# Row groups of the matmul array in a decoder trunk's mixer: neighbouring small matmuls put on different row groups and different banks

## The chip, the cores and the metric

One Trainium2 chip, one NeuronCore of it. The metric is device time in microseconds (us), the median of several executions. Engines are named as in the profile: PE is TensorE (matmul), PEld its weight load, DVE is VectorE, ACT is ScalarE, POOL is GpSimd, SP is SyncE, which issues most DMAs.

## What is computed

Two layers, each a mixer (RWKV-7 heads beside a pooling mixer) and a PEER expert FFN, on 512 tokens of width 1024. Only the mixer's recurrence matters here. Cut down, for each of 8 heads of size 64:

```python
def rwkv7_step(state, inp):
    r_t, w_t, k_t, v_t, kk_t, a_t = inp
    sa = jnp.einsum('bhvk,bhk->bhv', state, -kk_t)
    state = (state * w_t[:, :, None, :]
             + sa[..., None] * (kk_t * a_t)[:, :, None, :]
             + v_t[..., None] * k_t[:, :, None, :])
    y = jnp.einsum('bhvk,bhk->bhv', state, r_t)
    return state, y
_, ys = lax.scan(rwkv7_step, s0, (rh, wh, kh, vh, kk, ah))
```

## The kernel before

The kernel does not step through 512 tokens. It cuts them into 16 chunks of 32 (CH) and treats each chunk in closed form. Two heads of 64 rows share a tile of 128 partitions; such a pair is handled by `pair(p)`, p = 0 to 3. Four groups of 128 tokens (t = 0 to 3, NT = 4) each hold four chunks (cc = 0 to 3), one to each 32 partitions.

All matmuls named here have float32 operands; the profile shows two records of MATMUL for each. A matmul whose operands lie on 64 or 32 of the 128 partitions uses only those rows of the array (its row group); one whose output has 64 partitions uses only those columns. The steps that the change touches:

- **Triangular inputs** (L446 to L465). For each pair p and head h four matmuls of 64 rows (L454) fill one bank of PSUM; ACT (h = 0) and DVE (h = 1) copy its diagonal blocks out, and a DMA takes them to the forward substitution on DVE (L474 to L494).
- **Gram products** (`gram`, L618). Called for "ak", "rb" and "rkm", once for each head: four matmuls of 64 rows into one bank, then one masked DVE multiply (L625). Head 0 lies on rows 0 to 63, head 1 on rows 64 to 127.
- **Transitions** (`gmat(cc)`, L654). Once for each cc: four matmuls of 32 rows (row group cc) into one bank, then one DVE multiply (L661).
- **Chunk inputs** (`hmat(cc)`, L664). Once for each cc: eight matmuls of 64 rows and 64 columns into one bank, the two heads on different columns, then one ACT copy (L674). Rows 0 to 63 serve cc 0 and 1, rows 64 to 127 cc 2 and 3.
- Around them stand matmuls on all 128 rows: `transposed` (L601), `xm` (L632), `wu` (L641), `ypart` (L683, L684), and the recurrence over chunks, `chain(c)` (L694): one matmul (L703) and two DVE instructions (L704, L705) per step, 15 steps one after the other for each pair (14 with a matmul). `yout` (L708) has small 64x64 matmuls of its own.

Banks come from a pool of five ("ps"), a pool of two ("pss", every fourth request of `bank2`), and one for the chain ("psc").

The order of the work is set twice. The program writes it with `zipped`, which deals several lists of blocks out in proportion: the second part of pair p's blocks beside the chain of pair p-1, the output of pair p-2, the first part of pair p+1 and steps that accumulate the adaLN modulation on DVE (L197, eight instructions for each step). PRE = 12 says how many blocks of a pair make up its first part. Then the framework's scheduler orders the instructions on each engine (`schedule_with_timeline_sim=True`). [...]

Of the kernel before, what the change touches and what calls it, by code (L numbers as in the profile page):

```python
# [9 lines left out]
F32 = mybir.dt.float32  # L10
# [4 lines left out]
AF = mybir.ActivationFunctionType  # L15
ALU = mybir.AluOpType
# [3 lines left out]
P = 128  # L20
T = 512
NT = T // P
# [3 lines left out]
CH = 32  # L26
# [19 lines left out]
GEND = 4  # L46
PO = 1
FN, FM, FS = 3, 18, 8
PRE, EARLY = 12, True
G8B = 3  # L50
EG = 6
NROW = 6
# [56 lines left out]
def body(ctx, tc, A, tap=None):  # L109
    nc = tc.nc  # L110
    V, S, G, TE = nc.vector, nc.scalar, nc.gpsimd, nc.tensor
# [17 lines left out]
    def bank(shape=(P, T)):  # L129
        return psp[0].tile(list(shape), F32, tag="ps", name=nm("ps"))  # L130
# [4 lines left out]
    def s2t(name, shape=(P, T), dt=F32):  # L135
        return s2.tile(list(shape), dt, tag="s2", name=nm(name))

    def hht(name, shape=(P, T), dt=F32R):
        return hh.tile(list(shape), dt, tag="hh", name=nm(name))
# [9 lines left out]
    def C(n):  # L149
        o, w = COFF[n]  # L150
        return const[:, o:o + w]
# [8 lines left out]
    for l in range(L):  # L160
        v = pers.tile([P, NVEC], F32, name=f"vec{l}")
# [156 lines left out]
    def mixer(l):  # L318
        with ExitStack() as mctx:
# [79 lines left out]
            for t in range(NT):  # L399
                pt = bank()  # L400
# [44 lines left out]
                V.tensor_tensor(Pi, k, Pi, op=ALU.mult)  # L445
            for p in range(4):  # L446
                a, at = bt_[p], at_[p]
                for h in range(2):
                    hr = slice(h * 64, (h + 1) * 64)
                    hd = 2 * p + h  # L450
                    pt = bank((P, NT, P))
                    for t in range(NT):
                        ts_ = slice(t * P, (t + 1) * P)
                        TE.matmul(pt[:, t], at[hr, ts_], a[hr, ts_], start=True, stop=True)  # L454
                    for cc in range(4):
                        rows = slice(cc * CH, (cc + 1) * CH)
                        if h == 0:
                            S.activation(acmp[hd // 4][rows, hd % 4], pt[rows, :, rows], AF.Copy)
                        else:
                            V.tensor_copy(acmp[hd // 4][rows, hd % 4], pt[rows, :, rows])  # L460
                if p % 2 == 1:
                    for cc in range(4):
                        rows = slice(cc * CH, (cc + 1) * CH)
                        nc.sync.dma_start(ascr[cc, (p // 2) * 16:(p // 2 + 1) * 16].rearrange("i t s -> t i s"),
                                          acmp[p // 2][rows].rearrange("t h n s -> t (h n) s"))  # L465
# [101 lines left out]
            def bank2(shape=(P, T)):  # L567
                nb[0] += 1
                return sbank(shape) if nb[0] % 4 == 0 and not apart[0] else psp[0].tile(list(shape), F32, tag="ps", name=nm("ps"))
# [4 lines left out]
            def pair(p):  # L574
# [3 lines left out]
                z = {}  # L578
# [3 lines left out]
                def scaled(n, src):  # L582
                    def f():
                        if n == 0:
                            z["bk"] = [s2t("bk") for _ in range(2)]
                        pc = PC[:, p].rearrange("p (q s) -> p q s", s=2)
                        for j in range(2):
                            V.tensor_tensor(pairs(z["bk"][j])[:, :, j ^ n], pairs(src)[:, :, j], pc[:, :, j].unsqueeze(2).to_broadcast([P, NCH // 2, CH]), op=ALU.mult)
                    return f
# [6 lines left out]
                def transposed(n, src, outs=None):  # L596
                    def f():
                        s_ = z["bk"][n[1]] if n[0] == "bk" else z["vs"] if n == "UV" else src
                        pt = bank2((P, NT, P))
                        for t in range(NT):  # L600
                            TE.transpose(pt[:, t], s_[:, t * P:(t + 1) * P], ident)  # L601
                        if n == "AX":
                            for h in range(2):
                                z["AX", h] = q3("AX")
                                S.activation(z["AX", h][:, :, hrs[1 - h]], pt[:, :, hrs[h]], AF.Copy)
                        elif n == "vT":
                            for h in range(2):
                                S.activation(vz[p % 2][:, :, P * h:P * h + 64], pt[:, :, hrs[h]], AF.Copy)
                        elif n == "UV":
                            z[n] = [q3("UV") for _ in range(2)]  # L610
                            for j in range(2):
                                S.activation(z[n][j], pt, AF.Copy)
                        else:
                            z[n] = q3(n)
                            S.activation(z[n], pt, AF.Copy)
                    return f

                def gram(n, h, lh, rh, mk):  # L618
                    def f():
                        pt = bank2((P, NT, P))  # L620
                        for t in range(NT):
                            ts_ = slice(t * P, (t + 1) * P)
                            TE.matmul(pt[:, t], lh[hrs[h], ts_], rh[hrs[h], ts_], start=True, stop=True)
                        z[n, h] = hht(n, (P, NT, P), F32)
                        V.tensor_tensor(z[n, h], pt, C(mk).unsqueeze(1).to_broadcast([P, NT, P]), op=ALU.mult)  # L625
                    return f

                def xm(h):
# [7 lines left out]
                def wu(g):  # L636
                    def f():
                        pw = bank2((P, 2, 2, P))
                        for t in range(2):
                            for h in range(2):  # L640
                                TE.matmul(pw[:, t, h], Fb[:, 2 * p + h, 2 * g + t], z["AX", h][:, 2 * g + t], start=True, stop=True)  # L641
                        z["WU", g] = w = s2t("WU", (P, 2, 2, P))
                        beat[0] = S.activation(w, pw, AF.Copy)
                        u = w.rearrange("p t h c -> p t (h c)").rearrange("p t (b c) -> p t b c", c=64)[:, :, 0:4:3]
                        for cc in range(4):
                            rows = slice(cc * CH, (cc + 1) * CH)
                            out = z["UV"][cc % 2][rows, 2 * g:2 * g + 2].rearrange("p t (h c) -> p t h c", c=64)
                            (UENG[cc])(out, u[rows])
                    return f

                def W(t):
                    return z["WU", t // 2][:, t % 2].rearrange("p h c -> p (h c)")[:, 64:192]

                def gmat(cc):  # L654
                    def f():
                        rows = slice(cc * CH, (cc + 1) * CH)
                        pg = bank2((P, NT, P))
                        for t in range(NT):
                            TE.matmul(pg[:, t], W(t)[rows], z["bk", cc % 2][rows, t], start=True, stop=True, tile_position=(cc * CH, 0))
                        z["G", cc] = q3("G")  # L660
                        V.tensor_tensor(z["G", cc], pg, C("bones").unsqueeze(1).to_broadcast([P, NT, P]), op=ALU.mult)  # L661
                    return f

                def hmat(cc):  # L664
                    def f():
                        rows = slice(cc // 2 * 64, cc // 2 * 64 + 64)
                        ph = bank2((P, NT, 64))
                        for t in range(NT):
                            for h in range(2):
                                hr = hrs[h]  # L670
                                TE.matmul(ph[hr, t], z["bk", cc % 2][rows, t, hr], z["UV"][cc % 2][rows, t, hr], start=True, stop=True, tile_position=(cc // 2 * 64, h * 64))
                        if cc % 2 == 0:
                            z["H", cc // 2] = s2t("H", (P, 2, NT, 64))
                        S.activation(z["H", cc // 2][:, cc % 2], ph, AF.Copy)  # L674
                    return f

                def ypart(h):
                    def f():
# [3 lines left out]
                        for t in range(NT):  # L682
# [3 lines left out]
                        V.tensor_tensor(n3(rt)[hrs[h]], py[hrs[1 - h]], n3(rt)[hrs[h]], op=ALU.add)  # L686
                    return f

                blocks = [scaled(0, bt), scaled(1, kt), swapped, transposed("vT", v), gram("ak", 0, kt, at, "lt"), gram("ak", 1, kt, at, "lt"),
                          transposed("AX", at), transposed("UV", None), transposed(("bk", 0), None), transposed(("bk", 1), None), xm(0), xm(1),  # L690
                          gram("rb", 0, bt, rt, "le"), gram("rb", 1, bt, rt, "le"),
                          gram("rkm", 0, kt, rt, "le"), gram("rkm", 1, kt, rt, "le"), wu(0), wu(1), gmat(0), hmat(0), gmat(1), hmat(1), gmat(2), hmat(2), gmat(3), hmat(3), ypart(0), ypart(1)]

                def chain(c):  # L694
                    def f():
# [616 lines left out]
```

## Time and profile before

| what | value |
|---|---|
| median of 3 runs | 3503.16 us (3496.99 to 3510.04) |
| the profiled execution | 3505.42 us, its span 3503.7 us |
| mean granted PE clock | 0.94 of full |
| busy in the span | PE 94%, PEld 82%, DVE 80%, ACT 40%, POOL 25% |
| mixer of layer 0, from the triangular inputs to the last chain step | 131.7 to 413.5 us |
| mixer of layer 1, the same | 1852.1 to 2135.9 us |
| steps touched (L623, L659, L671) at work | 164 to 377 us and 1908 to 2094 us |

The page is of one execution. Time between the span and the run's own time (1.7 us) lies around the program. A matmul's end is modelled, so this text goes by the starts: the time from a matmul's start to the start of the next one of its list.

### The profile page before, as it was taken

Reading aid. Unit: us, or ns where it says so; the run is one execution under the profiler, and the core shown is the slowest. Engines: PE = TensorE matmul, PEld = TensorE weight load, DVE = VectorE, ACT = ScalarE, POOL = GpSimd, SP = SyncE. Lnnn points to the kernel's source line nnn. Section 1 sums busy time; section 2 is a strip of 40 time slices with the busy share of each in tenths; the row PEclk is TensorE's granted clock in tenths of the full one; section 3 lists DMA queues with packets and bytes.
Section 4 is the critical chain, followed back from the end, with each engine's and each line's share of the span. In section 5 each row is a group of like instructions: output and inputs, shape, how many; then the busy total and the mean of one; then the engine's idle time right before and its main releaser. Section 6 shows DMA issues by size and latency. Waiting matters only on the chain. (4 is left out here: it accounts for less than half of the span.)

```text
span 3503.7 us, 51112 instructions
## 1 busy us (share of the span) xinstructions
PE 3280.4 (94%) x18154; PEld 2870.3 (82%) x18154; DVE 2814.1 (80%) x6227; ACT 1389.2 (40%) x2228; POOL 869.7 (25%) x684
## 2 busy tenths in 40 slices
PE   5899898999999999999899998999999999999997
PEld 3778677999998888888777876889999888889886
DVE  5666479998877888899939654999898688888888
ACT  4433132345573334333353422334556543333333
POOL 2000000432202222556500000023331122245554
PEclk7977799999999999999999878999999999999998
DMA  5213244567789999999922232335767999999996
GB/s 192 76 55 99 72 163 139 154 196 262 265 289 354 334 343 347 356 381 399 360 72 85 73 97 83 119 118 161 265 238 276 325 327 343 339 341 355 350 369 260
DMA packets 361377, 826.41 MB, mean 236 GB/s; under 512 B 46496, under 2 KB 189600, under 8 KB 357792
## 3 DMA queue, kind: packets, MB, share of 16 engines
q1 hardware_dynamic: 287392, 554.68, 46.9%
q0 software_dynamic: 73728, 268.47, 20.3%
q8 instruction: 142, 2.33, 0.3%
q14 instruction: 115, 0.94, 0.1%
HBM read 730.75 MB, written 92.27 MB: 235 GB/s over the span
## 5 line engine op out<-in xcount | busy, mean ns | idle before, releaser
L277 PE MATMUL pss<-hi,wsp 128*128 128x384 f32 (+1 forms) x5168 | 1075.9, 359 | 97.0 <-DVE wsp L260 34.3
L1159 PE MATMUL ps<-vv,wg 128*128 128x512 f32 x4608 | 1078.8, 393 | 21.9 <-ACT vv L1142 6.8
L277 PEld LDWEIGHTS pss<-hi,wsp 128*128 128x128 f32 x5168 | 935.7, 194 | 171.6 <-DVE wsp L260 46.8
L1159 PEld LDWEIGHTS ps<-vv,wg 128*128 128x128 f32 x4608 | 867.3, 189 | 207.3 <-ACT vv L1142 11.4
L259 ACT ACTIVATE wsp<-raw 128x1024 fp32r<-128x1024 f32 x341 | 359.8, 1057 | 519.6 <-PE pss L277 409.1
L277 PE MATMUL pss<-lo,wsp 128*128 128x384 f32 (+1 forms) x2584 | 533.5, 347 | 0.0
L852 POOL DMA_INDIRECT row<-u,ex x256 | 314.3, 1228 | 845.7 <-DVE row L858 643.3
L260 DVE TENSOR_TENSOR wsp<-raw,wsp 128x1024 fp32r<-128x1024 f32 x341 | 431.6, 1267 | 67.2 <-ACT wsp L259 66.6
L277 PEld LDWEIGHTS pss<-lo,wsp 128*128 128x128 f32 x2584 | 461.4, 188 | 22.0 <-issue 0.5
L852 POOL DMA_INDIRECT row<-v,ex x256 | 332.2, 1298 | 243.9 <-DVE ox L866 191.6
L1143 DVE TENSOR_TENSOR vv<-raw,vv 128x512 fp32r<-128x512 f32 x512 | 345.1, 691 | 46.6 <-ACT vv L1142 42.0
L1142 ACT ACTIVATE vv<-raw 128x512 fp32r<-128x512 f32 x512 | 291.4, 619 | 112.2 <-DMA raw<-v 71.2
L858 DVE SCALAR_TENSOR_TENSOR row<-row,hx 128x1024 f32<-128x1024 f32 x256 | 318.0, 1248 | 13.9 <-DMA row<-u,ex 13.8
L866 DVE SCALAR_TENSOR_TENSOR ox<-row,wx,ox 128x1024 f32<-128x1024 f32 x254 | 325.1, 1280 | 2.5
L1133 ACT ACTIVATE wg<-ge 128x384 fp32r<-128x384 f32 x256 | 132.9, 524 | 487.9 <-DVE ge L1131 202.2
L968 POOL TENSOR_TENSOR eq<-eq,cid 128x400 f32<-128x400 f32 x128 | 181.6, 1438 | 478.4 <-DVE eq L966 341.2
L934 POOL TENSOR_TENSOR hf<-hi,lo 128x128 f32<-128x128 f32 x16 | 9.8, 624 | 991.3 <-DMA ada<-ada 923.6
L1134 DVE TENSOR_TENSOR wg<-ge,wg 128x384 fp32r<-128x384 f32 x256 | 141.0, 554 | 106.7 <-ACT wg L1133 94.4
L1043 ACT ACTIVATE gb<-ps 128x512 f32<-128x512 f32 x192 | 199.3, 1162 | 0.0
L1131 DVE TENSOR_TENSOR ge<-ge,g 128x192 f32<-128x192 f32 x496 | 156.7, 352 | 40.3 <-DMA g<-gscr 29.9
L1126 ACT ACTIVATE ge<-pss 128x384 f32<-128x384 f32 x80 | 39.2, 490 | 259.3 <-PE pss L277 255.1
L1022 DVE TENSOR_TENSOR oh<-oh,selg 128x1024 f16<-128x1024 f16 x96 | 71.1, 740 | 47.5 <-PE ps L1041 47.2
(451 smaller groups left out, 3307.6 us busy)
## 6 DMA issues: line engine op xcount, KB each, us to landing
raw<-uT SPq DMA_DIRECT2D x256, 512.0 KB
raw<-v SPq DMA_DIRECT2D x256, 512.0 KB
gscr<-gb SPq DMA_DIRECT2D x24, 2048.0 KB
g<-gscr SPq DMA_DIRECT2D x124, 384.0 KB
gespill<-ge SPq DMA_DIRECT2D x176, 192.0 KB
ge<-gespill SPq DMA_DIRECT2D x176, 192.0 KB
ada<-ada SPq DMA_DIRECT2D x96, 256.0 KB
raw<-ada SPq DMA_DIRECT2D x48, 512.0 KB
```

The costliest lines, as they stand in the source:

```text
L259: S.activation(w[:, 0], raw, AF.Copy)
L260: V.tensor_tensor(w[:, 1], raw, w[:, 0].bitcast(F32), op=ALU.subtract)
L277: TE.matmul(pt, w[:, a, k * P:(k + 1) * P], hs[k][b], start=start and n == 0, stop=stop and n == len(steps) - 1)
L852: G.indirect_dma_start(out=rows[n], out_offset=None, in_=A["u" if n < P else "v"], in_offset=bass.IndirectOffsetOnAxis(ap=ex[:, n % P:n % ...
L858: V.scalar_tensor_tensor(row, row, 1.0, hx, op0=ALU.mult, op1=ALU.mult, accum_out=dots[:, e:e + 1])
L866: V.scalar_tensor_tensor(ox, row, wx[:, e:e + 1], ox, op0=ALU.mult, op1=ALU.add)
L968: pace["G"] = G.tensor_tensor(eq, eq, z["id"][:, h].unsqueeze(1).to_broadcast([P, 8, NC]), op=ALU.mult)
L1043: S.activation(gb[:, :, o:o + 4].rearrange("p i t -> p t i"), pt, AF.Copy, scale=1.0 / GSC)
L1131: V.tensor_tensor(gq, gq, g[:, :, c % IG], op=ALU.mult)
L1142: S.activation(vv[0][q], raw[:, q * T:(q + 1) * T], AF.Copy)
L1143: vlo[q] = V.tensor_tensor(vv[1][q], raw[:, q * T:(q + 1) * T], vv[0][q].bitcast(F32), op=ALU.subtract)
L1159: end[0] = TE.matmul(acc[t][d2], wg[a][:, ts_], vv[b][d2], start=(c == 0 and a == 0 and b == 0), stop=(c == NK - 1 and a == 1))
```

## The change

The three kinds of products and the triangular inputs take all their banks first and then go over t with the heads (or the chunks) innermost, so that a matmul and the next one in the program use different row groups and different banks. `gram` does both heads in one block, `gmat` all four cc in one block, `hmat(s)` the two row halves b for one s (cc = 2b + s). The list of blocks is shorter by this (20 entries, not 28), and PRE goes from 12 to 11, which cuts the list at the same place as before. The number of matmuls, copies and DVE multiplies is the same, as are their shapes.

```diff
-PRE, EARLY = 12, True
+PRE, EARLY = 11, True
...
             for p in range(4):
                 a, at = bt_[p], at_[p]
+                both = [bank((P, NT, P)) for _ in range(2)]
+                for t in range(NT):
+                    ts_ = slice(t * P, (t + 1) * P)
+                    for h in range(2):
+                        hr = slice(h * 64, (h + 1) * 64)
+                        TE.matmul(both[h][:, t], at[hr, ts_], a[hr, ts_], start=True, stop=True)
                 for h in range(2):
-                    hr = slice(h * 64, (h + 1) * 64)
                     hd = 2 * p + h
-                    pt = bank((P, NT, P))
-                    for t in range(NT):
-                        ts_ = slice(t * P, (t + 1) * P)
-                        TE.matmul(pt[:, t], at[hr, ts_], a[hr, ts_], start=True, stop=True)
...
-                def gram(n, h, lh, rh, mk):
+                def gram(n, lh, rh, mk):
                     def f():
-                        pt = bank2((P, NT, P))
+                        pts = [bank2((P, NT, P)) for _ in range(2)]
                         for t in range(NT):
                             ts_ = slice(t * P, (t + 1) * P)
-                            TE.matmul(pt[:, t], lh[hrs[h], ts_], rh[hrs[h], ts_], start=True, stop=True)
-                        z[n, h] = hht(n, (P, NT, P), F32)
-                        V.tensor_tensor(z[n, h], pt, C(mk).unsqueeze(1).to_broadcast([P, NT, P]), op=ALU.mult)
+                            for h in range(2):
+                                TE.matmul(pts[h][:, t], lh[hrs[h], ts_], rh[hrs[h], ts_], start=True, stop=True)
+                        for h in range(2):
+                            z[n, h] = hht(n, (P, NT, P), F32)
+                            V.tensor_tensor(z[n, h], pts[h], C(mk).unsqueeze(1).to_broadcast([P, NT, P]), op=ALU.mult)
                     return f
...
-                def gmat(cc):
+                def gmat():
+                    pgs = [bank2((P, NT, P)) for _ in range(4)]
+                    for t in range(NT):
+                        for cc in range(4):
+                            rows = slice(cc * CH, (cc + 1) * CH)
+                            TE.matmul(pgs[cc][:, t], W(t)[rows], z["bk", cc % 2][rows, t], start=True, stop=True, tile_position=(cc * CH, 0))
+                    for cc in range(4):
+                        z["G", cc] = q3("G")
+                        V.tensor_tensor(z["G", cc], pgs[cc], C("bones").unsqueeze(1).to_broadcast([P, NT, P]), op=ALU.mult)
+
+                def hmat(s):
                     def f():
...
+                        phs = [bank2((P, NT, 64)) for _ in range(2)]
                         for t in range(NT):
...
+                            for b in range(2):
+                                rows = hrs[b]
+                                for h in range(2):
+                                    TE.matmul(phs[b][hrs[h], t], z["bk", s][rows, t, hrs[h]], z["UV"][s][rows, t, hrs[h]], start=True, stop=True, tile_position=(b * 64, h * 64))
```

What the scheduler makes of it is seen in the order of the instructions. **PE, layer 0, the Gram products rb and rkm of pair 0**, ahead of `wu` (rt, bt, kt are the tiles of r, b and k; ps and pss are banks). Before:

```order
L632 MATMUL ps_1507<-vz_394,ak_1467 128x64 x4
L623 MATMUL ps_1513<-rt_400,bt_445 128x128 x4
L623 MATMUL pss_1520<-rt_400,bt_445 128x128 x4
L623 MATMUL ps_1527<-rt_400,kt_576 128x128 x4
L623 MATMUL ps_1534<-rt_400,kt_576 128x128 x4
L641 MATMUL ps_1541<-AX_1400,Fb 128x128
```

and after:

```order
L635 MATMUL ps_1507<-vz_394,ak_1467 128x64 x4
L625 MATMUL ps_1513<-rt_400,bt_445 128x128
L625 MATMUL pss_1514<-rt_400,bt_445 128x128
L625 MATMUL ps_1513<-rt_400,bt_445 128x128
L625 MATMUL pss_1514<-rt_400,bt_445 128x128
L625 MATMUL ps_1513<-rt_400,bt_445 128x128
L625 MATMUL pss_1514<-rt_400,bt_445 128x128
L625 MATMUL ps_1513<-rt_400,bt_445 128x128
L625 MATMUL pss_1514<-rt_400,bt_445 128x128
L625 MATMUL ps_1527<-rt_400,kt_576 128x128
L625 MATMUL ps_1528<-rt_400,kt_576 128x128
```

Four matmuls of one head, then four of the other, have become head by head. Not everywhere: rb and rkm of pair 3 and ak of pairs 0 and 1 still stand as x4 and x4 in the new order of layer 0.

**PE, layer 0, transitions and chunk inputs of pair 0**, right behind `wu` (WU is its result, bk the scaled keys, UV the chunk's values). Before:

```order
L659 MATMUL ps_1563<-('bk', 0)243_1418,WU_1546 128x128 x2
L671 MATMUL ps_1570<-UV_1409,('bk', 0)243_1418 64x64 x4
L659 MATMUL ps_1581<-('bk', 1)245_1425,WU_1546 128x128 x2
L659 MATMUL ps_1598<-('bk', 0)243_1418,WU_1546 128x128 x2
L671 MATMUL pss_1588<-UV_1410,('bk', 1)245_1425 64x64 x4
L671 MATMUL ps_1605<-UV_1409,('bk', 0)243_1418 64x64 x4
L659 MATMUL ps_1563<-('bk', 0)243_1418,WU_1557 128x128 x2
L659 MATMUL ps_1581<-('bk', 1)245_1425,WU_1557 128x128 x2
L659 MATMUL ps_1598<-('bk', 0)243_1418,WU_1557 128x128 x2
```

and after:

```order
L662 MATMUL pss_1586<-('bk', 1)245_1425,WU_1546 128x128 x2
L674 MATMUL ps_1563<-UV_1409,('bk', 0)243_1418 64x64 x4
L674 MATMUL ps_1564<-UV_1409,('bk', 0)243_1418 64x64 x4
L662 MATMUL ps_1585<-('bk', 0)243_1418,WU_1546 128x128
L662 MATMUL ps_1587<-('bk', 0)243_1418,WU_1546 128x128
L662 MATMUL ps_1588<-('bk', 1)245_1425,WU_1546 128x128
L662 MATMUL ps_1585<-('bk', 0)243_1418,WU_1546 128x128
L662 MATMUL ps_1587<-('bk', 0)243_1418,WU_1546 128x128
L662 MATMUL ps_1588<-('bk', 1)245_1425,WU_1546 128x128
```

The scheduler had already mixed the two kinds before the change; now they change places less often, and three or four row groups follow each other one matmul at a time.

**DVE, layer 0, the masked copies of pair 1's transitions** (G<-ps), beside the chain of pair 0 (M, H) and an accumulation of the modulation (acc). Before:

```order
L661 TENSOR_TENSOR G_1746<-ps_1741,const 128x512
L195 TENSOR_SCALAR acc_1781<-raw_1782,silu_c 128x512
L661 TENSOR_TENSOR G_1803<-ps_1798,const 128x512
L197 SCALAR_TENSOR_TENSOR acc_1781<-raw_1782,silu_c,acc_1781 128x512
L705 TENSOR_TENSOR M_1670<-H_1579,psc_1730 128x64
```

and after:

```order
L708 TENSOR_TENSOR M_1657<-H_1583,psc_1763 128x64
L195 TENSOR_SCALAR acc_1767<-raw_1768,silu_c 128x512
L665 TENSOR_TENSOR G_1839<-ps_1819,const 128x512
L707 SCALAR_TENSOR_TENSOR H_1581<-M_1657,PC,H_1581 128x64
L665 TENSOR_TENSOR G_1841<-pss_1820,const 128x512
L665 TENSOR_TENSOR G_1843<-ps_1821,const 128x512
L665 TENSOR_TENSOR G_1845<-ps_1822,const 128x512
L197 SCALAR_TENSOR_TENSOR acc_1767<-raw_1768,silu_c,acc_1767 128x512
L708 TENSOR_TENSOR M_1657<-H_1581,psc_1806 128x64
```

Before, two of the four copies stood here and the other two 15 rows later; now all four stand together, with a step of the chain (M) behind them. On POOL nothing moves. On SP a few weight loads move by a few places, and on DVE some rows of the layer's later stages change places; the instructions themselves are the same.

More of the change, by code (lines that the diff above doesn't have):

```diff
@@ L457, in mixer @@
                         if h == 0:
-                            S.activation(acmp[hd // 4][rows, hd % 4], pt[rows, :, rows], AF.Copy)
+                            S.activation(acmp[hd // 4][rows, hd % 4], both[h][rows, :, rows], AF.Copy)
                         else:
-                            V.tensor_copy(acmp[hd // 4][rows, hd % 4], pt[rows, :, rows])
+                            V.tensor_copy(acmp[hd // 4][rows, hd % 4], both[h][rows, :, rows])
                 if p % 2 == 1:
@@ L655, in f @@
+                def hmat(s):
                     def f():
-                        rows = slice(cc * CH, (cc + 1) * CH)
-                        pg = bank2((P, NT, P))
+                        phs = [bank2((P, NT, 64)) for _ in range(2)]
                         for t in range(NT):
-                            TE.matmul(pg[:, t], W(t)[rows], z["bk", cc % 2][rows, t], start=True, stop=True, tile_position=(cc * CH, 0))
-                        z["G", cc] = q3("G")
-                        V.tensor_tensor(z["G", cc], pg, C("bones").unsqueeze(1).to_broadcast([P, NT, P]), op=ALU.mult)
@@ L662, in gmat @@
[L662 to L674, printed above, removed]
+                            for b in range(2):
+                                rows = hrs[b]
+                                for h in range(2):
+                                    TE.matmul(phs[b][hrs[h], t], z["bk", s][rows, t, hrs[h]], z["UV"][s][rows, t, hrs[h]], start=True, stop=True, tile_position=(b * 64, h * 64))
@@ L675, in hmat @@
+                        for b in range(2):
+                            if s == 0:
+                                z["H", b] = s2t("H", (P, 2, NT, 64))
+                            S.activation(z["H", b][:, s], phs[b], AF.Copy)
                     return f
@@ L687, in ypart @@
                     return f
-                blocks = [scaled(0, bt), scaled(1, kt), swapped, transposed("vT", v), gram("ak", 0, kt, at, "lt"), gram("ak", 1, kt, at, "lt"),
+                blocks = [scaled(0, bt), scaled(1, kt), swapped, transposed("vT", v), gram("ak", kt, at, "lt"),
                           transposed("AX", at), transposed("UV", None), transposed(("bk", 0), None), transposed(("bk", 1), None), xm(0), xm(1),
-                          gram("rb", 0, bt, rt, "le"), gram("rb", 1, bt, rt, "le"),
-                          gram("rkm", 0, kt, rt, "le"), gram("rkm", 1, kt, rt, "le"), wu(0), wu(1), gmat(0), hmat(0), gmat(1), hmat(1), gmat(2), hmat(2), gmat(3), hmat(3), ypart(0), ypart(1)]
+                          gram("rb", bt, rt, "le"), gram("rkm", kt, rt, "le"), wu(0), wu(1), hmat(0), gmat, hmat(1), ypart(0), ypart(1)]
                 def chain(c):
```

## Prediction

> **What bounds the kernel now.** First the page: how busy PE is, and the slices of the span with the granted clock.
>
> ```profile
> PE 3280.4 (94%) x18154; PEld 2870.3 (82%) x18154; DVE 2814.1 (80%) x6227; ACT 1389.2 (40%) x2228; POOL 869.7 (25%) x684
> PE   5899898999999999999899998999999999999997
> PEclk7977799999999999999999878999999999999998
> ```
>
> PE is the busiest engine, and the clock is low where the mixers stand: in slices 3 to 5 of 88 us each, and in slices 23 to 25 for layer 1. Next the table by stretches, from the first `wu` to the last products of pair 3 and on to the output projection, for both layers (columns: stretch, length, PE, PEld, DVE, ACT, POOL busy, then granted clock, DMA share, GB/s), and two short stretches inside the first.
>
> ```profile
> 226.00:384.00 158.00, 154.94 (x1134) 130.83 (x1133) 90.31 (x204) 48.05 (x107) 0.00 (x0) 0.73 0.26 83
> 384.00:428.00 44.00, 36.00 (x245) 26.93 (x243) 19.84 (x51) 5.41 (x10) 0.00 (x0) 0.81 0.05 17
> 1950.00:2103.00 153.00, 150.21 (x1142) 126.65 (x1142) 89.42 (x204) 49.49 (x110) 0.00 (x0) 0.77 0.28 85
> 236.00:257.00 21.00, 20.94 (x240) 18.35 (x239) 12.08 (x27) 12.25 (x30) 0.00 (x0) 0.99 0.01 2
> 291.00:311.00 20.00, 20.00 (x98) 15.19 (x97) 9.38 (x19) 2.35 (x6) 0.00 (x0) 0.50 0.25 79
> ```
>
> In these 158 and 153 us PE is busy for 98%, DVE for 57%, ACT for 30%. The clock is not 0.73: it is 0.99 or 0.50 by turns, and a mean in between. Who waits for whom from 226 to 384 us (us in total, times, longest):
>
> ```profile
> ACT H L674 <- PE ps L671: 29.0, 11, 5.3
> DVE M L705 <- PE psc L703: 21.5, 20, 3.8
> DVE G L661 <- PE ps L659: 9.1, 3, 5.7
> PE psc L703 <- DVE M L705: 3.0, 9, 0.5
> ```
>
> DVE and ACT wait for PE; PE waits 3.0 us in all. So PE's own list sets the time of this stage, and what it is spared there comes off the end, as far as the clock holds and no new wait comes.
>
> **How PE takes small matmuls.** The timeline of PE (start, length, line, xcount of records, two for each matmul): the triangular inputs of pairs 0 and 1, of pair 2, then Gram products, `gmat` and `hmat` of pair 0 at full clock, and one `gmat` alone at half clock.
>
> ```profile
> 131.70 2.82 PE L454 MATMUL ps<-bt,at 64*128 64x128 f32 x32
> 134.60 3.94 PE L277 MATMUL pss<-hi,wsp 128*128 128x512 f32 x16
> 140.28 1.71 PE L454 MATMUL ps<-bt,at 64*128 64x128 f32 x16
> 141.92 1.42 PE L277 MATMUL pss<-hi,wsp 128*128 128x512 f32 x5
> 245.38 0.82 PE L623 MATMUL ps<-rt,bt 64*128 64x128 f32 x5
> 245.94 0.37 PE L623 MATMUL pss<-rt,bt 64*128 64x128 f32 x1
> 236.48 0.71 PE L659 MATMUL ps<-('bk', 0)243_1418,WU 32*128 32x128 f32 x4
> 237.12 0.45 PE L671 MATMUL ps<-UV,('bk', 0)243_1418 64*64 64x64 f32 x8
> 237.50 0.37 PE L659 MATMUL ps<-('bk', 1)245_1425,WU 32*128 32x128 f32 x1
> 237.51 0.37 PE L659 MATMUL ps<-('bk', 0)243_1418,WU 32*128 32x128 f32 x1
> 237.71 0.27 PE L659 MATMUL ps<-('bk', 1)245_1425,WU 32*128 32x128 f32 x1
> 237.73 0.27 PE L659 MATMUL ps<-('bk', 0)243_1418,WU 32*128 32x128 f32 x1
> 354.82 2.07 PE L659 MATMUL ps<-('bk', 1)447_2289,WU 32*128 32x128 f32 x8
> 356.82 0.90 PE L671 MATMUL ps<-UV,('bk', 1)447_2289 64*64 64x64 f32 x10
> ```
>
> Two things are to be seen. Records of different row groups run side by side: at 237.50 and 237.51, again at 237.71 and 237.73, cc 1 and cc 2 start 10 to 20 ns apart, although the program has all of cc 1's four records first. And this reaches only so far: of two heads with eight records each, the second starts right behind the fifth record of the first (245.38 x5, then 245.94). So a row group seems to hold four records, one at work and three waiting, and only a fifth blocks those behind it. A group of x4 matmuls (8 records) is then half in the way of the next; x2 or x1 is not.
>
> One record costs a slot of 0.112 us at full clock: pair 2's 16 records take 5 + 8 = 13 slots, 1.64 us from 140.28 to 141.92, and pairs 0 and 1 in a row 3 x 5 + 8 = 23 slots, 2.90 us from 131.70 to 134.60; the difference, 1.26 us, is 10 slots plus 0.14. Taking 0.112, a stretch of one kind costs some 0.19 beside its slots, as does `gmat` at 236.48 (0.64 to the next start = 4 slots + 0.19). `hmat` has 64 columns and half the slot, 0.058: its eight records on two column halves (four slots) take 0.38 from 237.12 to 237.50, so 0.15 goes with the change of kind. At half clock the eight records at 354.82 take 2.00, twice 8 slots plus 0.2.
>
> [...]
>
> **The change part by part.** With this rule of four, the two orders of PE can be counted, slots on the longest row group and stretches of one kind.
>
> - *gmat*: layer 0 from 114 slots in 18 stretches to 69 in 13; layer 1 from 114 in 21 to 66 in 14. Spared: 45 x 0.112 + 5 x 0.19 = 6.0 us, and 48 x 0.112 + 7 x 0.19 = 6.7. It does not reach a quarter because the scheduler still breaks it with `hmat` and the chain.
> - *hmat*: from 139 slots in 25 stretches to 88 in 15, and from 136 in 25 to 91 in 15: 51 x 0.058 + 10 x 0.15 = 4.5, and 45 x 0.058 + 10 x 0.15 = 4.1.
> - *gram*: from 156 slots to 127, and from 159 to 126, stretches about the same: 29 x 0.112 = 3.2 and 33 x 0.112 = 3.7. Pair 3 and the early ak products gain nothing, their order is still x4 after x4.
> - Sum at full clock: 13.7 us and 14.5 us. The stage has 158 x 0.73 = 115.3 and 153 x 0.77 = 117.8 us of full-clock time, so 101.6 and 103.3 are left; at the same mean clocks 139.2 and 134.2 us, which is 18.8 less for each layer, **37.6 us**.
> - *Triangular inputs*: 10 slots, 1.1 us a layer. I take 0, because DVE decides there: its forward substitution follows its own copies of these banks. Bound: 2.2 us in all.
> - *Copies, multiplies, PRE*: the same instructions, the list cut at the same place: 0. DVE's 90 us of work still fit into 139 (65%). The tail (384 to 428 us, the last chain) holds none of the changed matmuls and moves as it is. Some DVE rows of later stages change places: 0, bound 6 us either way, one accumulation of eight of the rows below.
>
> *What is late next.* Four banks of `gmat` now fill together and are emptied one after the other by DVE, which also has the accumulations in its list, and PE's next blocks need these banks; and the chain's next matmul waits for M, now behind all four copies. The rows (mean ns third from the right, before the idle time):
>
> ```profile
> L661 DVE TENSOR_TENSOR G<-ps,const 128x512 f32<-128x512 f32 x14 | 9.4, 687 | 9.4 <-PE ps L659 9.1
> L197 DVE SCALAR_TENSOR_TENSOR acc<-raw,silu_c,acc 128x512 f32<-128x512 f32 x42 | 31.2, 744 | 2.2 <-DMA raw<-ada 1.9
> 398.07 0.69 PE L703 MATMUL psc<-M,G 128*128 128x64 f32 x2 [0.31 <-DVE M L705]
> 399.07 0.69 PE L703 MATMUL psc<-M,G 128*128 128x64 f32 x2 [0.31 <-DVE M L705]
> ```
>
> Four copies are 4 x 0.687 = 2.75 us. Of eight banks seven serve, so PE has three others meanwhile, and some 2 to 3 us of transposes and `hmat` in its list. A wait of 0 to 2.75 us for each of eight pairs, 0 to 22 us; I take 1 us, 8 us in all, since PE waits so little now. The chain alone needs 1.0 us a step at half clock (398.07, 399.07), 56 us for the 56 steps of a layer, far below 139.
>
> 37.6 - 8 = 29.6. From the profiled execution's 3505.4 that gives 3475.8; the median of the runs is 2.3 lower, so 3473.5: **3474 us**.
>
> **The rivals.**
>
> *A: the clock takes it back.* [...] With the mean 0.04 lower in both stages, 101.6 / 0.69 and 103.3 / 0.73 make 147.2 and 141.5, a gain of 22.3, with the waits 14: 3489. With 0.08 lower, 156.3 and 149.7, a gain of 5, with the waits -3: 3506. [...]
>
> *B: the banks.* If DVE's copies of a `gmat` stand behind a whole accumulation step, 0.5 + 7 x 0.744 = 5.7 us, PE stalls 5.7 + 2.75 = 8.4 for the six pairs that have such steps beside them, and 2.75 for two: 56 us against 37.6. That is 18 more than before: 3522 us. It decides from a wait of 37.6 / 8 = 4.7 us a pair. For it: M and the four copies now stand together in DVE's order. Against it: DVE waits for PE there, not the reverse, and the order has only one or two rows of an accumulation ahead of the copies. [...]
>
> *C: little changes, because PE already runs ahead enough.* If more of the overlap was there than my rule of four counts, only the spared stretches remain: 5 x 0.19 + 10 x 0.15 = 2.5 and 7 x 0.19 + 10 x 0.15 = 2.8 at full clock, 5.3 / 0.75 = 7 us: 3496. Against it: the x8 at 354.82 stood alone, with 8 full slots.
>
> **How the numbers follow.** Forecast 0.70, A 0.12, B 0.08, C 0.10. A change under 0.5% (17.5 us) is about what a measurement of this kernel can't tell from none, so faster means below 3485.6 and slower above 3520.7. The forecast lies below 3485.6 but for 0.06 (waits of over 2.5 us a pair); A is the same but for 0.01 slower; C is the same but for 0.02; B is slower. Faster 0.66, same 0.25, slower 0.09. The range goes from 3455 (no waits, 37.6 and 2.2 spared, the clock 0.02 higher, which is worth 7) to 3500 (C, and most of A); it leaves out B, a part of A, and 0.05 below.
>
> **What would show it.** In the profile after: pairs of starts of the two heads a few ns apart all through a Gram product; rb and rkm of pair 0 in some 16 slots, not 23; the way from the first `wu` to the last `ypart` of pair 3 at about 140 and 135 us, where it was 158 and 153; clocks of 0.73 and 0.77 for these; PE's waits for DVE at 3 to 7 us. Wrong it would be if the clock fell below 0.69, if PE waited for G, H or the Gram copies by tens of us, or if heads in turn did not start together.

## The result, and the profile after

The changed kernel takes 3440.6 us (median of 4 runs, 3438.1 to 3452.6) against 3502.6 us before (median of 4 runs beside it): 62 us less, a ratio of 0.9825, 95% interval 0.9802 to 0.9848. The forecast was 3474, 29 us less, with 3455 as the lower end. The sign was right, the size forecast was under half of what came, and the time lies below the range.

First the page of after: PE, and the granted clock in 40 slices.

```profile
PE 3211.2 (93%) x18154; PEld 2814.1 (82%) x18154; DVE 2809.3 (82%) x6227; ACT 1386.0 (40%) x2228; POOL 875.7 (25%) x684
PE   5889888999999999999899898999999999999997
PEclk7989899999999999999999888999999999999998
```

Slices 3 to 5 had a clock of 7 each and now have 8, 9 and 8; slices 23 to 25 had 8, 7 and 8 and now have 8 each. The stage from the first `wu` to the last `ypart` of pair 3, by the table of stretches (length, PE, PEld, DVE, ACT, POOL busy, granted clock, DMA share, GB/s), with the stretch ahead of it in layer 0 on top. Before:

```profile
164.30:232.80 68.50, 52.19 (x254) 45.43 (x253) 55.64 (x107) 17.74 (x35) 0.00 (x0) 0.75 0.22 66
232.80:382.50 149.70, 146.64 (x1085) 123.29 (x1085) 86.79 (x197) 46.69 (x104) 0.00 (x0) 0.74 0.27 85
1954.50:2101.40 146.90, 144.11 (x1085) 121.21 (x1085) 86.73 (x200) 46.81 (x105) 0.00 (x0) 0.76 0.29 87
```

After:

```profile
163.30:225.30 62.00, 46.18 (x254) 39.34 (x253) 55.06 (x109) 17.43 (x35) 0.00 (x0) 0.83 0.25 73
225.30:343.70 118.40, 111.89 (x1096) 95.13 (x1095) 86.59 (x202) 45.30 (x104) 0.00 (x0) 0.88 0.34 106
1922.10:2046.00 123.90, 115.60 (x1096) 97.64 (x1095) 87.41 (x205) 45.30 (x104) 0.00 (x0) 0.86 0.32 103
```

The stage is 31.3 us shorter in layer 0 and 23.0 in layer 1, 54.3 of the 67.3 us by which the profiled spans differ (3503.7 and 3436.4). The way up to layer 0's stage gives another 7.5 (the first `wu` starts at 225.3, it was 232.8), 6.5 of it in the stretch shown. The other 5.5 are a balance: between the two stages 6.4 are lost again, and behind layer 1's stage 11.9 are gained. No run took that rest apart.

How to split such a row. The traces of before and after hold no granted clock but 1.0 and 0.5, so 2 x (1 - clock) x length is the time at half clock: 77.8 and 70.5 us before, 28.4 and 34.7 after. Busy PE time x clock is the work in full-clock time: 108.5 and 109.5 before, 98.5 and 99.4 after (the clock has two digits, so some 0.7 us either way here, and 1.5 in the time at half clock). Length less PE is what PE waits: 3.1 and 2.8 before, 6.5 and 8.3 after. So work went down by 20.1 us and waits went up by 9.0, together 11.2; and 85.2 us less at half clock, of which half is time, made 42.6 (a slot takes 0.112 us at full clock, six from 238.07 to 238.74 after the change, and 0.213 at half, 355.20 to 355.41 before). The sum is 53.8 of the 54.3. Four fifths of the gain in the stage is clock.

The PE time of the three products themselves in this stage of layer 0 (columns as above, PE and PEld alone): `gmat`, `hmat` and Gram products, before

```profile
232.80:382.50 149.70, 25.48 (x128) 21.00 (x128) 0.74 0.27 85
232.80:382.50 149.70, 18.00 (x256) 13.81 (x256) 0.74 0.27 85
232.80:382.50 149.70, 16.83 (x129) 14.19 (x128) 0.74 0.27 85
```

and after

```profile
225.30:343.70 118.40, 11.95 (x128) 9.22 (x128) 0.88 0.34 106
225.30:343.70 118.40, 10.21 (x256) 7.74 (x256) 0.88 0.34 106
225.30:343.70 118.40, 11.93 (x130) 9.77 (x128) 0.88 0.34 106
```

`gmat` falls from 25.5 to 12.0 us, `hmat` from 18.0 to 10.2, the Gram products from 16.8 to 11.9. This is 26 of the 31 us, but it mixes slots and clock: all other matmuls of the stage, which the change leaves as they are, fall too, from 86.3 to 77.8 us. The timeline shows the slots alone. PE's timeline, after: four records of a `gmat`, then the rb product of pair 0 (start, length, line):

```profile
229.51 0.37 PE L662 MATMUL ps<-('bk', 0)243_1418,WU 32*128 32x128 f32 x1
229.51 0.37 PE L662 MATMUL pss<-('bk', 1)245_1425,WU 32*128 32x128 f32 x1
229.52 0.37 PE L662 MATMUL ps<-('bk', 0)243_1418,WU 32*128 32x128 f32 x1
229.53 0.37 PE L662 MATMUL ps<-('bk', 1)245_1425,WU 32*128 32x128 f32 x1
...
237.86 0.37 PE L625 MATMUL ps<-rt,bt 64*128 64x128 f32 x1
237.87 0.37 PE L625 MATMUL pss<-rt,bt 64*128 64x128 f32 x1
238.07 0.27 PE L625 MATMUL ps<-rt,bt 64*128 64x128 f32 x1
238.08 0.27 PE L625 MATMUL pss<-rt,bt 64*128 64x128 f32 x1
...
238.95 0.43 PE L706 MATMUL psc<-M,G 128*128 128x64 f32 x2
```

The four chunks start within 20 ns, the two heads 10 ns apart, as the change wants it. The rb product of pair 0 takes 1.09 us to the next start (237.86 to 238.95), 8 slots and a change of kind. What PE waits for in the stage, layer 0 and then layer 1 (us in total, times, longest), before

```profile
PE psc L703 <- DVE M L705: 3.0, 9, 0.5
PE psc L703 <- DVE M L705: 2.7, 8, 0.5
```

and after

```profile
PE psc L706 <- DVE M L708: 6.1, 12, 1.7
PE ps L674 <- ACT UV L572: 0.2, 1, 0.2
PE psc L706 <- DVE M L708: 7.6, 12, 3.6
```

The new waits are the chain's for M, 8.0 us in all. None is for a bank that a G, H or Gram copy holds; what else PE waited for comes to 0.2 us in layer 0 and 0.4 in layer 1.

### The profile page after: what moved, and what is told of

It reads as the page before. It is cut to its first block, busy times and chain, and to the rows that moved or that the text cites. A ratio compares the mean times of both kernels' runs of the same rounds, so it can differ in the third digit from the quotient of the medians.

```text
span 3436.4 us, 51106 instructions
## 1 busy us (share of the span) xinstructions
PE 3211.2 (93%) x18154; PEld 2814.1 (82%) x18154; DVE 2809.3 (82%) x6227; ACT 1386.0 (40%) x2228; POOL 875.7 (25%) x684
## 5 line engine op out<-in xcount | busy, mean ns | idle before, releaser
L1137 DVE TENSOR_TENSOR wg<-ge,wg 128x384 fp32r<-128x384 f32 x256 | 141.3, 555 | 104.6 <-ACT wg L1136 93.9
```

## The experiments

The question after this result was why the clock rose. Theory 1: row groups that work side by side count for the clock each for itself, so the packing raises it. Theory 2: it is the regrouped list, fewer and longer blocks of one kind, and not the turns. Theory 3 was named ahead of the first clock kernel too, and took the place of Theory 1 after it: the clock counts rows of the array in use times time, whoever uses them. A share below is just that: rows out of 128, times the time of the slots, over the time from burst to burst. Ratios come from the measurement with their interval and can lie up to 0.002 off the quotient of the two medians. Each clock kernel is one execution, whose stages are compared with each other.

**The clock by itself, first kernel.** Bursts of one kind and a DVE step in turn; n matmuls on all rows, on one group of 64 or on two in turn:

```
for copies in (1, 2):
    for burst, n in ((one, 4), (two, 8), (full, 4), (one, 8), (two, 16), (full, 8)):
        warm(24)
        for r in range(24):
            again(burst(n), copies)
```

> This kernel leaves the whole computation out and only measures the clock: twelve stages, each with 24 dense matmuls and then 24 bursts of small fp32 matmuls (128 columns each); after each burst one DVE step of 128x512 (or two) has to end before the next burst can start. In order: 4 matmuls of 64 rows on one row group, 8 matmuls in turn on two row groups, 4 matmuls of 128 rows, then 8, 16 and 8 of the same kinds; then all six again with two DVE steps. At 0.224 us a matmul a burst is 0.9 us (first three) or 1.8 us (last three) at full clock, the gap about 1.0 or 1.9 us, so the array is in use for about 0.47, 0.64, 0.32 and 0.49 of the time. Theory 1 (the clock counts row groups that work side by side each for itself): the stages with two row groups hold a mean clock of at least 0.9 where one row group with the same time in use falls to 0.5 to 0.8. Theory 2 (the clock only counts the time in use): one and two row groups have the same mean clock, within 0.05, in all four pairs. Theory 3 (it counts rows in use): 128 rows behave as two row groups do, and one row group has the lower clock.

The table of stretches, the six kinds with one DVE step (here the columns are PE, PEld, DVE, POOL, clock):

```profile
27.10:92.20 65.10, 47.06 (x193) 40.25 (x192) 15.90 (x23) 0.00 (x0) 0.54 0.00 1
115.60:179.60 64.00, 45.74 (x385) 39.15 (x384) 15.91 (x23) 0.00 (x0) 0.57 0.00 1
203.60:263.50 59.90, 41.87 (x193) 35.71 (x191) 15.90 (x23) 0.00 (x0) 0.63 0.00 1
286.60:392.10 105.50, 87.43 (x385) 80.47 (x384) 15.94 (x23) 0.00 (x0) 0.52 0.00 1
415.70:483.30 67.60, 49.32 (x769) 44.73 (x768) 15.91 (x23) 0.00 (x0) 1.00 0.01 1
504.80:571.90 67.10, 49.07 (x385) 44.56 (x383) 15.90 (x23) 0.00 (x0) 1.00 0.00 1
...
1067.70:1153.90 86.20, 49.27 (x769) 45.32 (x768) 31.80 (x46) 0.00 (x0) 1.00 0.00 1
1176.20:1261.30 85.10, 48.44 (x385) 44.49 (x383) 31.84 (x46) 0.00 (x0) 1.00 0.00 1
```

Row 4 and row 5 are the main reading. With 8 matmuls a burst on one row group PE is busy for 87.4 of 105.5 us (83%) and sits at half clock (0.52); with 16 on two groups in turn it is busy for 49.3 of 67.6 (73%) and has the full clock throughout (1.00). At full clock the two use PE for the same share of time: from start to start a burst takes 2.83 us in row 4 (286.61 to 289.44) and 2.85 in row 5 (418.57 to 421.42). The one group lost the clock in its second burst (0.52 over 105.5 us leaves some 4 us at full clock), the two groups never did. So busy time alone, Theory 2's rule in the expectation, does not give these two clocks. Nor do changes between kinds of matmuls, since a stage has none inside its bursts. And row 6, 128 rows with nothing side by side, has 1.00 as two groups do. Theory 1 held for this pair, but not for rows 1 and 2, where two groups fell as well (0.57, where it named 0.9), and it said nothing on 128 rows; Theory 3 agrees with all the rows of this table. In the last row 16 slots of 0.112 in a period of 3.62 us (1255.67 to 1259.30), a share of 0.49, still held the full clock (1.00). Row 3 shows it lost from below: its bursts of 8 slots start 1.94 us apart at full clock (215.14 to 217.08), a share of 0.46, and after eight of them it went to half clock (0.63 over the stage).

**The turns taken out, the blocks kept.** In all four products the loop over heads, chunks or halves goes outermost again; `gmat` for one:

```
-                    for t in range(NT):
-                        for cc in range(4):
+                    for cc in range(4):
+                        for t in range(NT):
```

> The changed kernel with the same blocks and banks, but the row groups one after the other again in every product (all of a head, of a chunk, of a half, then the next). Counted by the rule of four its list has 8.1 and 9.0 us more full-clock work in a layer than the changed kernel, and 7.3 and 7.0 less than before. Theory 1 (row groups side by side raise the clock): the clock of the stage is near that of before, 0.75, so the gain is 14.3/0.75 = 19 us: 0.9945 of before, about 3484 us. Theory 2 (the regrouping of the list into fewer and longer blocks is what lifted the clock, not the turns): most of the gain stays, clock 0.85 or more in the stage, 45 us or more faster than before, about 3457 us or less.

3464.9 us against 3508.9, a ratio of 0.9871 (0.9840 to 0.9902): 44 us, next to the 45 that Theory 2 named and far from the 19 of Theory 1.

```profile
226.70:361.00 134.30, 129.09 (x1095) 110.12 (x1095) 87.58 (x204) 45.48 (x104) 0.00 (x0) 0.81 0.30 95
1940.40:2068.40 128.00, 123.78 (x1095) 105.52 (x1095) 86.45 (x201) 45.30 (x104) 0.00 (x0) 0.85 0.31 97
```

The clock is 0.81 and 0.85, half-clock time 51.0 and 38.4. So the turns are not needed for a large part of the clock's gain; Theory 1 in its first form misses this. Work is 104.6 and 105.2, so 3.9 and 4.3 less than before, about half of what the rule of four counted.

**The parts alone.** Only the Gram products:

> Only the Gram products are changed, the rest is as before. Counted by the rule of four: 5.0 and 5.6 us less full-clock work in a layer. Theory 1 (work side by side raises the clock): the Gram products raise it where they stand, and the gain is twice the slots at 0.75 or more, 25 us: 3478 us. Theory 2 (clock stays as it was): 10.6/0.75 = 14 us, 3489 us.

3470.3 us, 0.9896 (0.9863 to 0.9928): 39 us less.

```profile
226.80:361.70 134.90, 132.47 (x1094) 112.27 (x1093) 87.40 (x203) 45.96 (x104) 0.00 (x0) 0.80 0.30 94
1944.10:2082.50 138.40, 135.72 (x1094) 114.58 (x1093) 87.74 (x203) 46.24 (x104) 0.00 (x0) 0.78 0.29 91
```

Only `gmat` and `hmat`:

> Only gmat and hmat are changed, the Gram products and triangular inputs are as before. Counted by the rule of four: 10.0 and 10.0 us less full-clock work in a layer. Theory 1 (work side by side raises the clock): most of the clock's part of the gain is here, since in the kernel before gmat and hmat lie mostly at half clock; 45 us, 3458 us, and gmat at full clock for most of its time. Theory 2 (clock stays as it was): 20/0.75 = 27 us, 3476 us.

3451.3 us, 0.9843 (0.9821 to 0.9865): 58 us less.

```profile
229.60:356.60 127.00, 119.95 (x1098) 102.21 (x1097) 88.23 (x206) 46.34 (x105) 0.00 (x0) 0.85 0.34 109
1932.20:2062.80 130.60, 122.37 (x1097) 104.44 (x1097) 88.08 (x206) 46.31 (x104) 0.00 (x0) 0.83 0.33 106
```

Each part gives more than its slots, because the clock rises with each (to 0.80 and 0.78, and to 0.85 and 0.83, from 0.74 and 0.76), and more than the 25 and 45 us of Theory 1. `gmat` in the second kernel stood at full clock for 51% and 42% of its time, not for most of it. The two parts add up to 97 us, where the whole change gave 62. The stage had 148 us at half clock before, so lifting all of it would give 74; what the first part lifts the second can't lift again.

**The triangular inputs alone.**

> Only the triangular inputs are changed. By the rule of four 1.1 us less full-clock work in a layer, beside DVE's own work. Forecast of the prediction: 0, at most 2.2 us less. [...]

3513.5 us against 3510.9, ratio 0.9996 (0.9972 to 1.0021). No difference, as forecast.

**More rows, no turns.** This separates Theory 3 from Theory 2 and from the slots, since the order is that of before:

```
-TE.matmul(pt[:, t], lh[hrs[h], ts_], rh[hrs[h], ts_], start=True, stop=True)
+TE.matmul(pt[:, t], lh[:, ts_], rh[:, ts_], start=True, stop=True)
...
-TE.matmul(pg[:, t], W(t)[rows], z["bk", cc % 2][rows, t], start=True, stop=True, tile_position=(cc * CH, 0))
+TE.matmul(pg[:, t], W(t), z["bk", cc % 2][:, t], start=True, stop=True)
```

> The kernel before, in its own order, but its Gram products and gmat take all 128 rows of their operands in place of 64 and 32 (so they add what does not belong in, and the mask of gmat is scaled by 0.001 to keep the numbers small). No work runs side by side here: by the rule of four the list loses 7.5 us of full-clock time in a layer, nearly all of it changes of kind between small and 128-row matmuls. Theory 3 (the clock counts rows in use times time): row-weighted work of the stage goes from 72 to 90 us, the half-clock time from the first wu to the last ypart falls from 79 and 72 us to under 30 in each layer, and with it 15 + 45 = 60 us: about 3445 us. Theory 2 (longer blocks in a new order lifted the clock): the order is that of before, so the clock stays at 0.75 and the gain is 15/0.75 = 20 us, 3487 us.

3445.8 us against 3510.9, 0.9799 (0.9759 to 0.9839): 65 us less, as much as the change itself.

```profile
227.40:343.10 115.70, 110.27 (x1085) 98.60 (x1084) 85.20 (x195) 46.71 (x104) 0.00 (x0) 0.98 0.35 110
1924.80:2050.60 125.80, 122.68 (x1084) 110.25 (x1083) 85.60 (x196) 46.70 (x104) 0.00 (x0) 0.88 0.32 101
```

Here the work did not shrink: 110.27 x 0.98 = 108.1 and 108.0 us, against 108.5 and 109.5 before. The 7.5 us a layer that the rule of four gave for the changes of kind came to 1 at most. Yet the stage is 34.0 and 21.1 us shorter, all of it from the clock: 4.6 and 30.2 us at half clock, before 77.8 and 70.5. Nothing more was put side by side here, so packing is not needed for the rise. The total met the expectation of Theory 3 with less work gained and more clock.

**Fewer rows, the turns kept.** The changed kernel with half of the rows in the Gram products and `hmat`:

```
-TE.matmul(pts[h][:, t], lh[hrs[h], ts_], rh[hrs[h], ts_], start=True, stop=True)
+TE.matmul(pts[h][:, t], lh[h * 64:h * 64 + 32, ts_], rh[h * 64:h * 64 + 32, ts_], start=True, stop=True, tile_position=(h * 64, 0))
...
-                                rows = hrs[b]
+                                rows = slice(b * 64, b * 64 + 32)
```

> The changed kernel, in its order, but its Gram products and hmat take only 32 of their 64 rows (half of each sum is left out). Slots and blocks stay the same, the row-weighted work of the stage falls from 72 to 65 us. Theory 3 (rows in use times time): the half-clock time from the first wu to the last ypart goes back from 27 and 34 us to 55 or more in each layer, which costs some 25 us: about 3466 us. Theory 2 (blocks and order set the clock): the time stays at 3441 us within 6.

3468.8 us, 0.9868 (0.9831 to 0.9905): 42 us less than before, where the change gave 62.

```profile
226.60:352.80 126.20, 121.44 (x1096) 102.40 (x1095) 84.97 (x199) 45.42 (x104) 0.00 (x0) 0.80 0.30 94
1933.70:2077.80 144.10, 136.38 (x1096) 114.54 (x1095) 87.84 (x205) 45.19 (x104) 0.00 (x0) 0.70 0.28 89
```

The work is, if anything, less than in the changed kernel (97.2 and 95.5 us), but the clock falls to 0.80 and 0.70, half-clock time 50.5 and 86.5, and the stage is 7.8 and 20.2 us longer. Slots say faster, the clock says slower, and the clock has it. The total met Theory 3's 3466; in layer 0 the half-clock time stayed a little below the 55 us that it named.

**The clock by itself, again.**

> Leaves the whole computation out and only measures the clock, with bursts of fp32 matmuls of 128 columns, 0.9 us of slots each at full clock, and one DVE step of 128x128 behind each, so that the array is in use for some 0.6 of the time. In order, each after 24 dense matmuls: one row group of 64 rows; two groups of 32 rows in turn; two of 64 in turn; four of 32 in turn; 128 rows; 128 rows with 64 output columns (three of four); then 128 rows with two, three, four DVE steps behind a burst (in use for less and less). At the end the 128 rows with one, two and three steps again, but started from half clock. Theory 3 (the clock counts rows in use times time, as the first clock kernel had it): one group of 64 and two of 32 (0.3 of rows and time) fall to half, two of 64, four of 32 and 128 rows hold full clock at 0.6; with 64 output columns full clock is held too; with more steps it is lost between 0.51 and 0.47, and from half clock it does not come back as long as the share stays below 0.65. Rival (it counts the number of records that start, whatever their rows): two groups of 32 hold the full clock as two of 64 do, and 128 rows do not.

This one missed: the dense matmuls, which depended on no burst, ran in the gaps between the bursts, and the full clock there tells nothing (the mean over the whole run is 0.787, and 0.728 with them tied). With them tied to the DVE step:

> The second clock kernel again, with the dense matmuls between the stages tied to the DVE step before them, so that they can't fill the gaps between bursts. Leaves the whole computation out. Bursts of fp32 matmuls of 128 columns, 0.9 us of slots at full clock (plus 0.1 for a change of kind), and one DVE step of 128x128 behind each, about 0.5 us with its waits, so in use for some 0.65 of the time; 36 bursts a stage. In order: one row group of 64 rows; two of 32 in turn; two of 64 in turn; four of 32 in turn; 128 rows; 128 rows with 64 output columns (three of four); then 128 rows with two, three and four DVE steps. At the end 128 rows with one, two and three steps started from half clock. Theory 3 (rows in use times time): one group of 64 and two of 32 (share 0.32) at half clock; two of 64, four of 32 and 128 rows (share 0.65) at full clock; 64 output columns at full clock too; with more steps full clock is lost between a share of 0.51 and 0.47. Rival (records that start are counted, whatever their rows): two groups of 32 hold full clock as two of 64 do, and 128 rows do not. Whether output columns count is open: if they do, the stage with 64 columns (share 0.65 x 0.62 = 0.40) goes to half clock.

The first seven stages, in the order of the expectation, and below the dots the first two of those that start from half clock (each has twelve bursts of the one group of 64 ahead, which take the clock down):

```profile
28.30:113.40 85.10, 71.68 (x289) 61.43 (x288) 10.21 (x35) 0.00 (x0) 0.52 0.00 1
137.40:222.90 85.50, 71.76 (x576) 61.55 (x576) 10.19 (x35) 0.00 (x0) 0.52 0.00 1
246.80:302.20 55.40, 41.67 (x576) 34.84 (x576) 10.19 (x35) 0.00 (x0) 1.00 0.01 2
324.30:382.70 58.40, 42.16 (x1153) 35.36 (x1152) 10.19 (x35) 0.00 (x0) 1.00 0.01 3
404.80:459.70 54.90, 41.48 (x289) 34.67 (x288) 10.22 (x35) 0.00 (x0) 1.00 0.00 1
481.80:541.50 59.70, 46.28 (x289) 33.27 (x288) 10.22 (x35) 0.00 (x0) 1.00 0.00 1
563.50:644.30 80.80, 53.23 (x290) 45.80 (x288) 20.43 (x70) 0.00 (x0) 0.76 0.00 0
...
949.80:1036.10 86.30, 68.28 (x385) 57.76 (x384) 13.72 (x47) 0.00 (x0) 0.80 0.00 1
1058.20:1186.10 127.90, 95.25 (x385) 82.47 (x384) 23.95 (x82) 0.00 (x0) 0.52 0.00 0
```

64 rows alone and two groups of 32 in turn: half clock (0.52 each). Two groups of 64, four of 32, and 128 rows: full clock (1.00 each). Two groups of 32 have as many records as two of 64 (x576), so the number of records does not make this difference. The sixth stage, with 64 output columns in three of four matmuls, keeps the full clock (1.00): the columns made no difference here. In the seventh, with a second DVE step, 8 slots stand in a period of 1.87 us at first and of 1.93 from 574.66 on, a share of 0.46, until the clock goes:

```profile
601.67 1.13 PE L100 MATMUL pb<-mv,x 128*128 128x128 f32 x8 [0.80 <-DVE mv L117]
603.60 1.13 PE L100 MATMUL pb<-mv,x 128*128 128x128 f32 x8 [0.80 <-DVE mv L117]
605.53 1.77 PE L100 MATMUL pb<-mv,x 128*128 128x128 f32 x8 [0.80 <-DVE mv L117]
608.10 2.04 PE L100 MATMUL pb<-mv,x 128*128 128x128 f32 x8 [0.80 <-DVE mv L117]
```

Its clock is 0.76: full for a little over half of the stage, and then lost. With three and four steps it was 0.54 and 0.52. So full clock was kept at a mean share of 0.49 (the last row of the first clock kernel) and lost at 0.46.

Winning it back took more than keeping it. From half clock, with a slot of 0.213, 128 rows with one DVE step (bursts 2.46 us apart, a share of 0.69) came back to full after five bursts (0.80 over the stage); with two steps (2.85 us, 0.60) they stayed at 0.50 for the 99 us to the end of the stage.

The traces of the two kernels say when the clock changes. All 79 gaps before and all 91 after, from one change of the granted clock to the next, are multiples of 3.41 us (from 236.49 to 379.85 us before: 20.5, 17.1, 17.1, 20.5, 6.8, 13.7, 17.1, 17.1, 6.8 and 6.8 us). Take the share by these steps of 3.41 us, as an estimate from the starts, slots and rows of PE's records. In the stage of before all ten losses of the full clock follow steps of 0.29 to 0.41, and all eleven returns follow steps of 0.63 to 1.00. The two ranges are not limits: one step of 0.41 lost nothing, and one of 0.83 brought nothing back. After the change four of nine losses follow steps of 0.43 to 0.53. Each of the ten losses before was followed by 6.8 to 20.5 us at half clock.

## Why the prediction was wrong, by its steps

| Kernel | us at half clock, L0 and L1 | Full-clock work, us | Time against its before |
|---|---|---|---|
| before | 77.8, 70.5 | 108.5, 109.5 | 1 |
| Gram products alone | 54.0, 60.9 | 106.0, 105.9 | 0.9896 |
| serial | 51.0, 38.4 | 104.6, 105.2 | 0.9871 |
| gmat and hmat alone | 38.1, 44.4 | 102.0, 101.6 | 0.9843 |
| after | 28.4, 34.7 | 98.5, 99.4 | 0.9825 |
| half the rows | 50.5, 86.5 | 97.2, 95.5 | 0.9868 |
| 128 rows, old order | 4.6, 30.2 | 108.1, 108.0 | 0.9799 |

- **The failed step** is "at the same mean clocks 139.2 and 134.2 us". The clocks did not stay at 0.73 and 0.77: over the prediction's own stretches, which start 7 and 5 us ahead of the first `wu` and end 2 us later, they became 0.89 and 0.87. The spared work and the new waits alone, 11.2 us at full clock, would at the old clocks be 11.2/0.75 = 15 us of the stage's 54; the rest came with the clock.
- **The clock's sign.** The forecast let the clock stay, rival A had it fall by 0.04 or 0.08, and a rise stood only as 0.02 in the lower end of the range, worth 7 us. The first clock kernel shows the opposite of A: 0.52 for one group of 64 and 1.00 for two in turn, with PE busy for 83% and 73%. The packed products have the same rows times records in less time, so their share rises: a `gmat` that stood alone on one group of 32 rows, as at 354.82, used a quarter of the rows, and now uses up to all of them (four chunks from 229.51 to 229.53). What was spared was time at a quarter or a half of the rows, the very time that pulled the share down. The two kernels that change the rows show it from both sides: more rows with the same work, 65 us faster; fewer rows with less work, 28 us of stage slower than after. A row of the prediction had it already: from 291 to 311 us PE is busy for 20.00 of 20.00 us at a clock of 0.50, so the low clock there did not come with little busy time.
- **The slots** were counted somewhat too high: 28.2 us at full clock by the rule of four. From each record's start to the next, less idle time, times the clock of the moment, summed over the records of both layers, 24.2 were spared: `gmat` gave 4.9 and 5.9 (forecast 6.0 and 6.7), `hmat` 2.6 and 3.3 (4.5 and 4.1), the Gram products 3.3 and 4.2 (3.2 and 3.7). In the stage itself, where some of the Gram products don't lie, PE's work fell by 20.1. The change of kind is the likely part that was too dear: `hmat` was to save 1.5 by it, and the kernel with 128 rows, which removes most changes of kind, saved almost nothing. That it is this was not tested by itself.
- **The waits** were right in size and in part by luck: 8 us forecast, 8.0 measured, though the 1 us a pair was a choice between 0 and 2.75, and all of it is for M in the chain, none for banks. So rival B had no part.
- **Rival C** is out: the three products were spared 24.2 us of full-clock time, where C had 5.3.
- **The signs named:** the two heads did start together, rb did take 8 slots, and PE's waits for DVE, 6.1 and 7.6 us, lie near the upper end of the 3 to 7 named and just above it. The stage, forecast at 140 and 135 us from 158 and 153, came to 127 and 130 by the same stretches (118 and 124 by the narrower ones above), and the clocks of 0.73 and 0.77 did not hold.
- **Triangular inputs at 0** held.
- **What stays open.** Half-clock time doesn't follow the full-clock work of the table alone: serial has more work than `gmat` and `hmat` alone, and less half-clock time in layer 1. That it depends on how low-row blocks and chain steps lie together in the steps of 3.41 us is the author's guess, and no run took that apart. So serial's 44 us are not explained beyond this: it has fewer and longer blocks of a kind, its work fell by 4 us a layer, and its clock rose to 0.81 and 0.85.

## What to carry to other kernels

When a matmul stage shows a mixed clock, ask first how many rows of the array its matmuls use over time, and not only how busy PE is: here 83% busy on 64 rows had a clock of 0.52, and 73% busy on two such groups in turn had 1.00. A change that packs small-row matmuls can then be worth its slots and the clock of everything around them: here its price at the old mean clock, less the waits, came to 15 of the stage's 54 us. Split a stage into work, waits and half-clock time before and after; the three terms tell at once which of them moved.

## What the runs showed of the hardware

- With the same slots a burst and one DVE step behind each (clock3), the granted clock was 0.52 for one group of 64 rows and for two of 32, and 1.00 for two of 64, four of 32 and 128 rows. With 64 output columns in three of four matmuls it was 1.00 too, and two groups of 32 and two of 64 have the same 576 records.
- On 128 rows the full clock was kept at a mean share of 0.49 (1.00 over the stage, clock1) and lost at 0.46 (0.63 over the stage, clock1; 0.76, clock3). In the traces of before and after its changes lay multiples of 3.41 us apart; by the estimate from slots and rows the ten losses in the stage of before follow steps of 0.29 to 0.41.
- Four 32-row matmuls on four row groups start within 20 ns (229.51 to 229.53 in the rows above), and two of 64 rows 10 ns apart (237.86 and 237.87).
